# Projection operands by feature block: 256 tokens' high and low parts, then 320 tokens' high and low parts

## The chip, the cores and the metric

One core of a Trainium2 chip. The metric is device time in microseconds (us) of one execution, the median over several; "span" is the time from the first to the last instruction in the profiler's records of one execution. Engines: TensorE (PE; PEld is its loading of weights), VectorE (DVE), ScalarE (ACT), GpSimd (POOL) and SyncE (SP), which issues the transfers.

## The reference

One layer of a streaming encoder, in float32, on 512 prompt tokens and 64 sample tokens, with model width 1024:

```python
h = x + W_out [ GDN_group(n) ; DiffAttn_group(n) ]    # n = rmsnorm(x), one combined input projection of n
h = h + MemCrossAttn(rmsnorm(h), per-layer memory K/V)
h = h + W2 relu(W1 rmsnorm(h))^2
y = rmsnorm_final(h)
```

GDN is a gated delta rule over chunks of 64 tokens (four heads of 128 by 128 state) with a short convolution ahead; DiffAttn is causal attention by chunks with two softmax maps a head, of which the second is subtracted; MemCrossAttn attends to 256 memory rows with four heads of 256; the feed-forward layer has 4096 hidden features. Outputs are y and the new keys, values, states and memory projections.

## The kernel before

All 576 tokens (T; 512 of the prompt and 64 of the sample) are processed together, with features on the 128 partitions and tokens along the free dimension. Matmuls run in a reduced float32 form, so each weight and each input is kept as a high and a low part, and a product is made of three: high by high, high by low, low by high.

The inputs of a projection lie in tiles from `pair` (L79): 128 partitions by 2 parts by 4 feature blocks by 576 tokens, so that the low part of a feature block lies 4 x 576 columns behind its high part. Two such tiles hold the 1024 features of an input: xs for the normalised x, oa and ob for the outputs of the scan and of the diff attention, hx for the normalised h ahead of memory attention, mo for its output, fx for the input of the feed-forward layer, and one tile sx for each group of 512 hidden features.

`project` (L165) makes 128 output features of all tokens, in two halves of the tokens, `HALVES` = (0, 256) and (256, 320), each in one PSUM bank. For the first half, `high_parts` (L181) reads high and low of 256 tokens with one matmul of 512 columns, and a second matmul of 256 columns multiplies the low weights. For the second half three matmuls of 320 columns do it. This repeats for each of 8 feature blocks (4 in the second feed-forward matrix). After a half, the given `evac` adds the two halves of the bank and what else it has to do; `split_to` (L193) writes high and low parts of a result for a later projection: ScalarE casts the high part (L197), VectorE subtracts it from the source (L198), or with a gain the lines L200 and L201.

The stages, in time: projections of n (with `first_half`, L302, for the first ones), five groups of chunks of the scan, between which projections are laid, the last of them the sample's chunk ("the last scan chunk" below); then four diff-attention heads, during which the rest of the projections and then those of the memory keys and values (`wh` blocks by 512 weight columns, input as the stationary operand) fill TensorE; then the output projection w_out with the residual in hT, memory attention head by head (L1026 normalises a score row, L1044 and L1045 split its output, one PSUM bank g0 for the prompt tokens and one, g1, for the sample), the projection w_mem_o, and the feed-forward layer in 8 groups. Weights are loaded by SyncE into three `raw` buffers and split by ScalarE (L157) and VectorE (L158).

A scheduler of the framework orders the instructions of each engine from the program, by its own priorities and costs and by buffers coming free; `issue_after` and `keep_in_program_order` fix a few. So an instruction that is split in two also moves others. In the last scan chunk the lines are: L692 subtracts what the state predicts from the values (in the tile on), L697 forms the new values vn, L713 updates the state S, L718 to L724 normalise the chunk's output (again in a tile on), and the splits of oa follow it.

Of the kernel before, what the change touches and what calls it, by code (L numbers as in the profile page):

```python
# [15 lines left out]
P = 128  # L16
# [18 lines left out]
def hybrid_layer_kernel(  # L35
# [129 lines left out]
    def project(w, x, evac, kt=KT, halves=HALVES, between=None):  # L165


        for a0, n in halves:
            b = bank("pr")
            for k in range(kt):  # L170
                low_part = lambda: mm(b[:, :n], w[1][:, k, :], x[k // 4][:, 0, k % 4, a0 : a0 + n], start=False, stop=False)
# [20 lines left out]

    def split_to(x, src, k, a0, g=None):  # L193

        h, lo = (x[k // 4][:, j, k % 4, a0 : a0 + src.shape[-1]] for j in range(2))
        if g is None:
            A.copy(h, src)  # L197
            V.tensor_tensor(lo, src, h.bitcast(F32), ALU.subtract)  # L198
# [42 lines left out]
    xs = [pair(i, F32R) for i in (0, 1)]  # L241
    w2 = w_in[0]
    grow = small("B1", [1, 4 * P])
    grow2 = small("B1", [1, 4 * P])
# [35 lines left out]
    def hi(t, qs=(0, 1)):  # L280
        t0, n = TT[t]
        for q in qs:
            A.copy(xs[q][:, 0, :, t0 : t0 + n], turned[t][q])

    def lo(t, qs=(0, 1)):
        t0, n = TT[t]
        for q in qs:
            V.tensor_tensor(  # L288
                xs[q][:, 1, :, t0 : t0 + n], turned[t][q], xs[q][:, 0, :, t0 : t0 + n].bitcast(F32), ALU.subtract
            )  # L290

    class Parts(list):
# [9 lines left out]
    def first_half(m):  # L302

        b = bank("pr")
        for k in range(KT - 1):
            high_parts(b, wts[m][0], xs, k, 0, 256)
        for k in range(KT):
            mm(b[:, :256], wts[m][1][:, k, :], xs[k // 4][:, 0, k % 4, :256], start=False, stop=False)
        high_parts(b, wts[m][0], xs, KT - 1, 0, 256)
        return b  # L310

# [429 lines left out]
            project_z()  # L741
        S = gdn_scan(c, c0, t0, n, prepared[c], S)
    nc.sync.dma_start(o_gdn_s[0, 0].rearrange("h k v -> k h v"), S)
    oa = pair(2, F32R)
    for h in range(H):
        split_to((oa,), cq[:, h, :], h, 0)


    with tc.issue_after(opened[mybir.EngineType.DVE]):
# [143 lines left out]
        finish = diff_head(h, finish)  # L893
    finish()

    ob = pair(5, F32R)
    for h in range(H):
        split_to((ob,), od[:, h, :], h, 0)


    mkv = pair(1)
# [73 lines left out]
        return r2  # L975


    hx = [pair(i, F32R) for i in (4, 3)]
# [20 lines left out]
    for h in range(H):  # L999
        qh = [small("kd" if h % 2 else "aT", [P, T]) for i in range(2)]  # L1000
        for i in range(2):
            def scaled(b, a0, n, more):
                q = qh[i][:, a0 : a0 + n]
                if more is not None:
                    add_to(q, b, more)
                    b = q
                V.tensor_tensor(q, b, rB[:, a0 : a0 + n], ALU.mult)

            project(
                weights(w_mem_q[0], (2 * h + i) * P), hx, scaled,  # L1010
                between=broadcast if h == i == 0 else None,
            )
        pT = [small("p1" if h % 2 else "vb", [P, T]) for _ in range(2)]
        for t, (q0, _) in enumerate(QT):
            t0, n = TT[t]
            kk = mkT if t < 4 else cmT
            b = bank()
            for i in range(2):
                mm(b[:, :NMEM], qh[i][:, q0 : q0 + P], kk[:, 2 * h + i, :], start=i == 0, stop=i == 1)
            mx, l = tiny([P, 1]), tiny([P, 1])  # L1020
            V.tensor_reduce(mx, b[:, :NMEM], AX.X, ALU.max)
            V.tensor_scalar(mx, mx, -1.0 / 16, None, ALU.mult)
            p = small("p0", [P, 512])
            A.activation(p[:, :NMEM], b[:, :NMEM], AF.Exp, bias=mx, scale=1.0 / 16, accum_out=l)
            V.reciprocal(l, l)
            V.tensor_scalar(p[:, :NMEM], p[:, :NMEM], l, None, ALU.mult)  # L1026
            bt = bank()
            for bi in range(2):
                tr(bt[:, bi * P : (bi + 1) * P], p[:, bi * P : (bi + 1) * P])
            A.copy(pT[0][:, t0 : t0 + n], bt[:, P - n : P])  # L1030
            V.tensor_copy(pT[1][:, t0 : t0 + n], bt[:, 2 * P - n : 2 * P])
        if h % 2 == 0:
            mo.append(pair(4 if h else 5, F32R))
        for i in range(2):
            b, b2 = bank("g0"), bank("g1")
            fs = slice((2 * h + i) * P, (2 * h + i + 1) * P)
            for bi in range(2):
                mm(b, mv[:, bi, fs], pT[bi][:, :SEQ], start=bi == 0, stop=bi == 1)
            for bi in range(2):
                mm(b2[:, :DEC], cmv[:, bi, fs], pT[bi][:, SEQ:], start=bi == 0, stop=bi == 1)  # L1040
            j = 2 * (h % 2) + i
            for src, ts_ in ((b, slice(0, SEQ)), (b2[:, :DEC], slice(SEQ, T))):
                dh, dl = (mo[h // 2][:, p, j, ts_] for p in range(2))
                A.copy(dh, src)  # L1044
                V.tensor_tensor(dl, src, dh.bitcast(F32), ALU.subtract)  # L1045

    fx = [pair(i, F32R) for i in (3, 2)]
# [5 lines left out]

    NG = 8
    def ff1(g):
        sx = (pair((4, 1, 5)[g % 3], F32R),)
        for i in range(4):
            def evac(b, a0, n, more):
                f = small("fs", [P, 320])[:, :n]
                if more is not None:  # L1060
                    add_to(f, b, more)
                    b = f
                V.tensor_tensor(f, b, rB[:, a0 : a0 + n], ALU.mult)  # L1063
                V.scalar_tensor_tensor(f, f, 0.0, f, ALU.max, ALU.mult)  # L1064
# [132 lines left out]
```

## Time and profile before

| | before |
|---|---|
| median of 3 runs (us) | 1063.34 |
| lowest to highest (us) | 1062.84 to 1063.38 |
| profiled execution (us) | 1061.57 |
| its span (us) | 1059.5 |
| granted clock, mean | 0.996 |
| matmuls | 6574 |
| HBM traffic | 79.14 MB read, 9.74 MB written |

A line of a group gives source line, engine, operation, output and inputs by the program's names, shapes, the count after the x, then the busy time in us and the mean ns of one, and at the end the idle time of the engine just before such instructions with what ended it. A line of a timeline gives the start in us, the time from the first start to the last end of a run of equal instructions, and the same names; in brackets stands the idle time before it, and what ended it. Tiles of a pool are named without their numbers, and one slot's name, u, stands for most of the tiles from `pair`.

### The profile page before, as it was taken

To read this page: it belongs to the slowest core of one execution; us is meant where nothing else is said; L and a number is where in the kernel's file an instruction comes from. 1 tells how busy PE (TensorE), PEld (TensorE's weight loads), DVE (VectorE), ACT (ScalarE), POOL (GpSimd) and SP (SyncE) were. 2 spreads that over 40 slices of the span, in tenths; PEclk is the share of its full clock that TensorE was granted. 3 is DMA by queue.
4 is the path that set the end of the run, shared out by engine and by line. 5 is a ranking of instruction groups with operands and counts; after the bars stand their busy time and mean duration, and the time that the engine had idled before them with its cause. 6 is when DMAs were issued, how large, how long until landed. Compare 5 with 4: busy or idle time off the path is not lost.

```text
span 1059.5 us, 16941 instructions
## 1 busy us (share of the span) xinstructions
PE 1034.8 (98%) x6574; PEld 929.9 (88%) x6574; DVE 671.5 (63%) x1471; ACT 432.6 (41%) x897; POOL 73.8 (7%) x126
## 2 busy tenths in 40 slices
PE   8999899999999999999999999999999999999997
PEld 6999898898788877999887799999999999999996
DVE  6767684756467575564555666666666666666674
ACT  6644754333265665343333443323232323222344
POOL 4411120311000000000000000000000000000000
PEclk9999999999999999999999999999999999999998
DMA  7332310100132255524211122132414141323312
GB/s 212 116 120 78 114 41 21 42 1 22 54 88 63 89 179 198 166 80 140 60 41 40 57 83 63 58 100 60 116 47 124 44 119 50 110 59 109 91 51 90
DMA packets 139442, 89.96 MB, mean 85 GB/s; under 512 B 5522, under 2 KB 130576, under 8 KB 138852
## 3 DMA queue, kind: packets, MB, share of 16 engines
q1 hardware_dynamic: 138996, 88.24, 28.0%
q8 instruction: 52, 0.85, 0.3%
q10 hardware_dynamic: 368, 0.66, 0.2%
q14 instruction: 26, 0.21, 0.1%
HBM read 79.14 MB, written 9.74 MB: 84 GB/s over the span
## 4 chain that ended last, share of the span: by engine, by line
PE 90%; issue 4%; DVE 2%; ACT 2%; POOL 1%; DMA 0%; POOLq 0%; ACTq 0%; DVEq 0%
PE pr L103 70%; PE g L103 10%; PE gs L103 3%; PE ba L109 3%; PE ba L103 2%; PE g L109 2%; POOL tg L204 1%; POOL tiny L204 0%; PE pr L109 0%; PE gs L109 0%; ACT wh L157 0%; ACT u L1109 0%; ACT Y L656 0%; POOL u L630 0%; DVE on L724 0%
## 5 line engine op out<-in xcount | busy, mean ns | idle before, releaser
L103 PE MATMUL pr<-u,wh 128*128 128x512 f32 (+1 forms) x2664 | 699.5, 343 | 1.2 <-DVE u L288 0.9
L103 PEld LDWEIGHTS pr<-u,wh 128*128 128x128 f32 x2664 | 456.5, 188 | 37.8 <-issue 1.7
L103 PE MATMUL pr<-u,wl 128*128 128x256 f32 (+1 forms) x1776 | 484.7, 299 | 0.0
L103 PEld LDWEIGHTS pr<-u,wl 128*128 128x128 f32 x1776 | 328.4, 189 | 8.0 <-DVE wl L355 0.3
L157 ACT CAST wh<-raw 128x1024 fp32r<-128x1024 f32 (+1 forms) x153 | 136.5, 892 | 231.2 <-PE pr L103 212.4
L158 DVE TENSOR_TENSOR wl<-raw,wh 128x1024 fp32r<-128x1024 f32 (+1 forms) x153 | 157.4, 1029 | 61.3 <-ACT wh L157 59.5
L943 DVE TENSOR_TENSOR u<-u,pr 128x256 f32<-128x256 f32 (+1 forms) x160 | 72.3, 452 | 62.8 <-PE pr L103 60.2
L204 POOL TENSOR_TENSOR tiny<-tiny,nhalf 128x1 f32<-128x1 f32 (+4 forms) x11 | 10.1, 918 | 664.1 <-DVE tiny L1127 409.3
L197 ACT CAST u<-p 128x256 fp32r<-128x256 f32 x64 | 27.8, 435 | 51.8 <-DVE p L1064 51.8
L103 PE MATMUL pr<-wh,u 128*128 128x512 f32 x128 | 42.6, 405 | 0.0
L198 DVE TENSOR_TENSOR u<-p,u 128x256 fp32r<-128x256 f32 x64 | 29.2, 457 | 15.2 <-ACT u L197 15.2
L190 ACT COPY p<-pr 128x256 f32<-128x256 f32 (+1 forms) x44 | 16.4, 373 | 51.3 <-PE pr L103 51.3
L191 DVE TENSOR_TENSOR p<-pr,p 128x256 f32<-128x256 f32 (+1 forms) x44 | 18.6, 422 | 26.9 <-ACT p L190 26.9
L945 DVE TENSOR_TENSOR u<-u,pr 128x256 f32<-128x256 f32 x80 | 33.6, 420 | 2.4
L1063 DVE TENSOR_TENSOR p<-pr,rB 128x320 f32<-128x320 f32 x32 | 15.7, 492 | 25.7 <-PE pr L103 25.7
L415 DVE SCALAR_TENSOR_TENSOR p<-p,gcol,p 128x579 f32<-128x579 f32 x33 | 27.1, 821 | 6.4 <-ACT p L413 5.9
L1064 DVE SCALAR_TENSOR_TENSOR p<-p 128x256 f32<-128x256 f32 x64 | 29.3, 458 | 2.2
L665 ACT COPY X<-g 128x512 f32<-128x512 f32 (+1 forms) x24 | 13.2, 550 | 42.6 <-PE g L109 42.5
L200 ACT ACTIVATE u<-u,gcol 128x256 fp32r<-128x256 f32 (+1 forms) x32 | 17.0, 534 | 31.1 <-DVE u L945 31.1
L103 PE MATMUL g<-u,qz 128*128 128x256 f32 (+4 forms) x96 | 29.5, 411 | 0.0
L103 PEld LDWEIGHTS pr<-wh,u 128*128 128x128 f32 x128 | 23.6, 188 | 4.5 <-issue 0.2
L634 DVE SCALAR_TENSOR_TENSOR B<-lev,At 128x512 f32<-128x512 f32 (+1 forms) x30 | 20.7, 696 | 10.6 <-PE g L103 8.8
(317 smaller groups left out, 1211.8 us busy)
## 6 DMA issues: line engine op xcount, KB each, us to landing
raw<-in_w_ff_dram SPq DMA_DIRECT2D x32, 512.0 KB
raw<-in_w_ff_dram SPq DMA_DIRECT2D x64, 256.0 KB
raw<-in_w_in_dram SPq DMA_DIRECT2D x28, 512.0 KB
raw<-in_w_mem_k_dram SPq DMA_DIRECT2D x8, 512.0 KB
raw<-in_w_mem_v_dram SPq DMA_DIRECT2D x8, 512.0 KB
raw<-in_w_out_dram SPq DMA_DIRECT2D x8, 512.0 KB
raw<-in_w_mem_q_dram SPq DMA_DIRECT2D x8, 512.0 KB
raw<-in_w_mem_o_dram SPq DMA_DIRECT2D x8, 512.0 KB
```

Of the source, the lines that this page charges most:

```text
L103: i = nc.tensor.matmul(out, lhsT, rhs, start=start, stop=stop)
L109: i = nc.tensor.transpose(out, in_, ident[:n, :n])
L157: A.copy(wh, raw)
L158: V.tensor_tensor(wl, raw, wh.bitcast(F32), ALU.subtract)
L197: A.copy(h, src)
L198: V.tensor_tensor(lo, src, h.bitcast(F32), ALU.subtract)
L204: G.tensor_tensor(out, in_, bc(nhalf[: in_.shape[0], 0:1], list(in_.shape)), ALU.pow)
L415: V.scalar_tensor_tensor(yv[:, :n], cb[:, i : i + n], cwt[:, m, i : i + 1], yv[:, :n], ALU.mult, ALU.add)
L634: V.scalar_tensor_tensor(B[:n, :, :n], lev[:n, :n].unsqueeze(1).to_broadcast([n, 4, n]), float(lv), At[:n, :, :n], ALU.is_equal, ALU.mult,)
L943: V.tensor_tensor(hm, hm, b, ALU.add)
L945: V.tensor_tensor(hm, hm, more, ALU.add)
L1064: V.scalar_tensor_tensor(f, f, 0.0, f, ALU.max, ALU.mult)
```

## The change

A tile of a projection's inputs is now [128 partitions, 4 feature blocks, 1152 columns]. Within a feature block lie 256 tokens' high parts, the same tokens' low parts, 320 tokens' high parts and their low parts. The 512 columns that the first half's matmul reads are neighbours. `piece` finds a stretch of one part; a stretch may not cross from the first 256 tokens to the rest, so the splits of oa and ob, which took 576 tokens at once, are done by halves, and the split of a memory-attention output takes its 512 prompt tokens with one cast (which writes two separate pieces) and two subtracts.

```diff
+    def operand(slot):
+        return up.tile([P, 4, 2 * T], F32R, tag=f"u{slot}", name=nm("x"))
+
+    def piece(u, j, k, a0, n):
+        at = 256 * j + a0 if a0 < 256 else 512 + 320 * j + a0 - 256
+        return u[:, k, at : at + n]
...
     def high_parts(b, w, x, k, a0, n, kt=KT):
-        xk = x[k // 4][:, :, k % 4, a0 : a0 + n]
+        xk = x[k // 4]
         if a0 == 0:
-            mm(b.rearrange("p (j n) -> p j n", j=2), w[:, k, :], xk, start=k == 0, stop=k == kt - 1)
+            mm(b, w[:, k, :], xk[:, k % 4, :512], start=k == 0, stop=k == kt - 1)
         else:
-            mm(b[:, :n], w[:, k, :], xk[:, 0], start=k == 0, stop=False)
-            mm(b[:, :n], w[:, k, :], xk[:, 1], start=False, stop=k == kt - 1)
+            mm(b[:, :n], w[:, k, :], piece(xk, 0, k % 4, a0, n), start=k == 0, stop=False)
+            mm(b[:, :n], w[:, k, :], piece(xk, 1, k % 4, a0, n), start=False, stop=k == kt - 1)
...
     def split_to(x, src, k, a0, g=None):
-        h, lo = (x[k // 4][:, j, k % 4, a0 : a0 + src.shape[-1]] for j in range(2))
+        h, lo = (piece(x[k // 4], j, k % 4, a0, src.shape[-1]) for j in range(2))
...
-    oa = pair(2, F32R)
+    oa = operand(2)
     for h in range(H):
-        split_to((oa,), cq[:, h, :], h, 0)
+        for a0, n in HALVES:
+            split_to((oa,), cq[:, h, a0 : a0 + n], h, a0)
...
-    ob = pair(5, F32R)
+    ob = operand(5)
     for h in range(H):
-        split_to((ob,), od[:, h, :], h, 0)
+        for a0, n in HALVES:
+            split_to((ob,), od[:, h, a0 : a0 + n], h, a0)
...
-            for src, ts_ in ((b, slice(0, SEQ)), (b2[:, :DEC], slice(SEQ, T))):
-                dh, dl = (mo[h // 2][:, p, j, ts_] for p in range(2))
-                A.copy(dh, src)
-                V.tensor_tensor(dl, src, dh.bitcast(F32), ALU.subtract)
+            blk = mo[h // 2][:, j]
+            dh = blk[:, :1024].rearrange("p (c n) -> p c n", c=2)[:, :, :256]
+            A.copy(dh, b.rearrange("p (c n) -> p c n", c=2))
+            for a0 in (0, 256):
+                V.tensor_tensor(
+                    piece(mo[h // 2], 1, j, a0, 256), b[:, a0 : a0 + 256],
+                    piece(mo[h // 2], 0, j, a0, 256).bitcast(F32), ALU.subtract,
+                )
+            dh, dl = (piece(mo[h // 2], p, j, SEQ, DEC) for p in range(2))
+            A.copy(dh, b2[:, :DEC])
+            V.tensor_tensor(dl, b2[:, :DEC], dh.bitcast(F32), ALU.subtract)
...
```

The other tiles (xs, hx, fx, sx) change from `pair` to `operand`, and the lines that write or read them use `piece`. Lines behind the new functions have numbers higher by 7, later ones by up to 17.

Every projection keeps its matmuls and their number. The program order of the engines moves at three places. The first is VectorE in the last scan chunk. The rows of before, from L692 on (tg holds small factors, gs a bank of the scan, vb its values):

```order
L692 TENSOR_TENSOR on_2659<-vb_2487,gs_2654 64x512
L697 TENSOR_TENSOR vn_2666<-gs_2661,tg_2445 64x512
L719 TENSOR_REDUCE tg_2686<-on_2688 64x4
L720 TENSOR_TENSOR tg_2686<-tg_2686,tg_2478 64x4
L721 TENSOR_SCALAR tg_2686<-tg_2686 64x4
```

and of after (x_2703 is oa, u_78 holds the scan's output):

```order
L700 TENSOR_TENSOR on_2659<-vb_2487,gs_2654 64x512
L205 TENSOR_TENSOR x_2703<-u_78,x_2703 128x256 x4
L705 TENSOR_TENSOR vn_2666<-gs_2661,tg_2445 64x512
L727 TENSOR_REDUCE tg_2686<-on_2688 64x4
L728 TENSOR_TENSOR tg_2686<-tg_2686,tg_2478 64x4
```

Four subtracts of 256 tokens now stand between on and vn. On ScalarE the same stretch, before (u_2703 is oa; pr, zr and wh belong to projections between):

```order
L190 COPY u_78<-pr_3155 128x256
L718 ACTIVATE on_2688<-gs_2668 64x512
L157 CAST wh_3454<-raw_3452 128x1024
L190 COPY zr_3238<-pr_3221 128x256
L197 CAST u_2703<-u_78 128x576 x4
```

and after:

```order
L197 COPY u_78<-pr_3163 128x256
L204 CAST x_2703<-u_78 128x256 x4
L726 ACTIVATE on_2688<-gs_2668 64x512
L164 CAST wh_3462<-raw_3460 128x1024
L197 COPY zr_3246<-pr_3229 128x256
L204 CAST x_2703<-u_78 128x320 x4
```

The casts of the first 256 tokens stand ahead of the activation on the chunk's output, those of the rest where all stood.

The second place is TensorE from the end of the scan through the diff attention, where projection matmuls and attention matmuls are interleaved anew, with the same matmuls in all. The third is the last head of memory attention on TensorE, before (g_1088 and g_1090 are the bank g0 for the prompt tokens, p the probabilities, ba a transpose, pr_5902 the first bank of w_mem_o, u_5665 the first tile of mo):

```order
L103 MATMUL g_1088_5874<-p_1061_5792,u_4187 128x512
L103 MATMUL g_1088_5874<-p_1062_5793,u_4187 128x512
L109 MATMUL ba_5869<-ident,p_1086_5865 128x128 x2
L103 MATMUL g_1089_5875<-p_1061_5792,u_5025 128x64
L103 MATMUL g_1090_5884<-p_1061_5792,u_4187 128x512
L103 MATMUL g_1089_5875<-p_1062_5793,u_5025 128x64
L103 MATMUL g_1090_5884<-p_1062_5793,u_4187 128x512
L103 MATMUL g_1091_5885<-p_1061_5792,u_5025 128x64
L103 MATMUL g_1091_5885<-p_1062_5793,u_5025 128x64
L103 MATMUL pr_5902<-u_5665,wh_5898 128x512
```

and after (x_5685 is the first tile of mo):

```order
L110 MATMUL g_1088_5896<-p_1061_5814,u_4203 128x512
L110 MATMUL g_1088_5896<-p_1062_5815,u_4203 128x512
L116 MATMUL ba_5891<-ident,p_1086_5887 128x128 x2
L110 MATMUL g_1089_5897<-p_1061_5814,u_5041 128x64
L110 MATMUL pr_5926<-x_5685,wh_5922 128x512
L110 MATMUL g_1089_5897<-p_1062_5815,u_5041 128x64
L110 MATMUL pr_5926<-x_5685,wl_5923 128x256
L110 MATMUL pr_5984<-x_5685,wh_5980 128x512
L110 MATMUL g_1090_5907<-p_1061_5814,u_4203 128x512
L110 MATMUL g_1090_5907<-p_1062_5815,u_4203 128x512
L110 MATMUL g_1091_5908<-p_1061_5814,u_5041 128x64
L110 MATMUL g_1091_5908<-p_1062_5815,u_5041 128x64
```

Three matmuls of w_mem_o now stand ahead of the second use of bank g0.

More of the change, by code (lines that the diff above doesn't have):

```diff
@@ L170, in project @@
             for k in range(kt):
-                low_part = lambda: mm(b[:, :n], w[1][:, k, :], x[k // 4][:, 0, k % 4, a0 : a0 + n], start=False, stop=False)
+                low_part = lambda: mm(b[:, :n], w[1][:, k, :], piece(x[k // 4], 0, k % 4, a0, n), start=False, stop=False)
                 if k == kt - 1:
@@ L239, in turn @@
         return b.rearrange("p (i t) -> p i t", i=4)[:, :, :n]
-    xs = [pair(i, F32R) for i in (0, 1)]
+    xs = [operand(i) for i in (0, 1)]
     w2 = w_in[0]
@@ L282, in hi @@
         for q in qs:
-            A.copy(xs[q][:, 0, :, t0 : t0 + n], turned[t][q])
+            A.copy(piece(xs[q], 0, slice(0, 4), t0, n), turned[t][q])
     def lo(t, qs=(0, 1)):
@@ L288, in lo @@
             V.tensor_tensor(
-                xs[q][:, 1, :, t0 : t0 + n], turned[t][q], xs[q][:, 0, :, t0 : t0 + n].bitcast(F32), ALU.subtract
+                piece(xs[q], 1, slice(0, 4), t0, n), turned[t][q], piece(xs[q], 0, slice(0, 4), t0, n).bitcast(F32),
+                ALU.subtract,
             )
@@ L975, in norm_columns @@
         return r2
-    hx = [pair(i, F32R) for i in (4, 3)]
+    hx = [operand(i) for i in (4, 3)]
     for m in range(KT):
@@ L1032, in hybrid_layer_kernel @@
         if h % 2 == 0:
-            mo.append(pair(4 if h else 5, F32R))
+            mo.append(operand(4 if h else 5))
         for i in range(2):
@@ L1041, in hybrid_layer_kernel @@
             j = 2 * (h % 2) + i
-            for src, ts_ in ((b, slice(0, SEQ)), (b2[:, :DEC], slice(SEQ, T))):
-                dh, dl = (mo[h // 2][:, p, j, ts_] for p in range(2))
-                A.copy(dh, src)
-                V.tensor_tensor(dl, src, dh.bitcast(F32), ALU.subtract)
-    fx = [pair(i, F32R) for i in (3, 2)]
+            blk = mo[h // 2][:, j]
[9 more added lines that the diff above has]
+            V.tensor_tensor(dl, b2[:, :DEC], dh.bitcast(F32), ALU.subtract)
+    fx = [operand(i) for i in (3, 2)]
     for m in range(KT):
@@ L1055, in ff1 @@
     def ff1(g):
-        sx = (pair((4, 1, 5)[g % 3], F32R),)
+        sx = (operand((4, 1, 5)[g % 3]),)
         for i in range(4):
```

2 lines of the change are left out of this document (1 added, 1 removed).

## The prediction

> **What bounds the kernel now.** I read the page first: the busy shares, the chain that ended last and the granted clock.
>
> ```profile
> span 1059.5 us, 16941 instructions
> PE 1034.8 (98%) x6574; PEld 929.9 (88%) x6574; DVE 671.5 (63%) x1471; ACT 432.6 (41%) x897; POOL 73.8 (7%) x126
> PEclk9999999999999999999999999999999999999998
> PE 90%; issue 4%; DVE 2%; ACT 2%; POOL 1%; DMA 0%; POOLq 0%; ACTq 0%; DVEq 0%
> ```
>
> TensorE is busy for 98% of the span and makes 90% of the chain, at full clock in every slice. So the time changes only if a matmul of the same shape follows the one before it sooner, or if TensorE idles more or less. How much idle there is, and where, the windows say (window, length, then busy time of PE, PEld, DVE, ACT and POOL, the clock, the DMA share and GB/s):
>
> ```profile
> 285.00:431.00 146.00, 143.96 (x815) 118.71 (x814) 94.78 (x262) 85.36 (x240) 6.47 (x8) 1.00 0.40 126
> 515.00:594.00 79.00, 75.25 (x394) 58.87 (x394) 39.81 (x118) 26.64 (x74) 0.00 (x0) 1.00 0.12 34
> 636.00:1034.00 398.00, 397.37 (x2500) 373.18 (x2501) 261.69 (x517) 120.21 (x211) 1.17 (x1) 1.00 0.28 80
> ```
>
> TensorE idles 146.00 - 143.96 = 2.04 us from the last scan chunk's tail to the end of the memory projections, 79.00 - 75.25 = 3.75 us in memory attention, and 0.63 us in 398 us of feed-forward.
>
> **The 512-column read.** The groups by shape give the matmuls whose moving operand becomes contiguous (count after the x, then total us and mean ns; a mean includes pipeline latency and isn't the spacing). The last row is the matmul that alternates with them.
>
> ```profile
> L103 PE MATMUL pr<-u,wh 128*128 128x512 f32 x888 | 330.5, 402 | 0.9 <-DVE u L288 0.9
> L103 PE MATMUL pr<-u,u 128*128 128x512 f32 x32 | 10.8, 397 | 0.0
> L103 PE MATMUL pr<-u,wl 128*128 128x256 f32 x888 | 231.0, 287 | 0.0
> ```
>
> Sixteen more stand in the views of the tiles kd and wab, whose rows name the shapes at the end:
>
> ```profile
> L103 PE MATMUL pr<-u,kd x24: 309/309/503, 22.4 to 35.8; 128*128 128x320 f32 x16, 128*128 128x512 f32 x8
> ```
> ```profile
> L103 PE MATMUL pr<-u,wab x24: 305/309/398, 97.1 to 101.1; 128*128 128x320 f32 x16, 128*128 128x512 f32 x8
> ```
>
> That is 888 + 32 + 8 + 8 = 936 matmuls of 6574. None is added or removed. Each reads 256 high and then 256 low columns; before, the low ones lie 4 x 576 x 4 = 9,216 B behind, after, they follow at once. What a break in the middle costs shows where the trace has both kinds in a row. In the memory projections the moving operand is a weight block of 512 neighbouring columns; in the first projections the two-piece operand comes several times in a row (start, us from first start to last end, tiles, count):
>
> ```profile
> 412.01 0.62 PE L103 MATMUL pr<-wh,u 128*128 128x512 f32 x2
> ...
> 414.05 0.62 PE L103 MATMUL pr<-wh,u 128*128 128x512 f32 x2
> ```
> ```profile
> 18.68 1.08 PE L103 MATMUL pr<-u,wh 128*128 128x512 f32 x4
> 19.59 1.12 PE L103 MATMUL pr<-u,wl 128*128 128x256 f32 x8
> ```
>
> Contiguous: nine starts in 414.05 - 412.01 = 2.04 us, 226.7 ns each. In two pieces: these four matmuls end 1.08 us after the first began, and one alone takes 0.40, so (1.08 - 0.40) / 3 = 226.7 ns each. The same, so I price the break at 0. The 256-column ones are (1.12 - 0.28) / 7 = 120 ns apart, with 0.28 for one alone (a row at 109.83, below).
>
> In a projection the two shapes alternate, and there a pair should take 226.7 + 120 = 346.7 ns. The timeline of two projections, which read the same two-piece tiles:
>
> ```profile
> 103.64 0.40 PE L103 MATMUL pr<-u,wh 128*128 128x512 f32 x1
> ...
> 105.03 0.40 PE L103 MATMUL pr<-u,wh 128*128 128x512 f32 x1
> ```
> ```profile
> 109.59 0.40 PE L103 MATMUL pr<-u,wh 128*128 128x512 f32 x1
> 109.83 0.28 PE L103 MATMUL pr<-u,wl 128*128 128x256 f32 x1
> ...
> 111.36 0.40 PE L103 MATMUL pr<-u,wh 128*128 128x512 f32 x1
> ```
>
> The first runs four pairs in 1.39 us, 347.5 ns each; the second five in 1.77 us, 354.0 each. The second pace loses 354.0 - 346.7 = 7.3 ns a pair, and if that loss were the break, removing it would give at most 936 x 7.3 = 6.8 us. But the first keeps nearly the nominal pace with the same break. The loss comes from something else in a stream without bubbles, and I leave it where it is: term 0, other end -6.8.
>
> [...]
>
> **Splits by half, last scan chunk.** The splits of the scan's output (oa) become four casts and four subtracts of 256 tokens, then four of 320, and the program order places the first group inside the scan's last chunk: on VectorE between L692 (on) and L697 (vn), on ScalarE ahead of L718. What stands there now:
>
> ```profile
> 277.67 0.68 DVE L692 TENSOR_TENSOR on<-vb,gs 64x512 f32<-64x512 f32 x1 [0.19 <-PE gs L103]
> 279.76 0.68 DVE L697 TENSOR_TENSOR vn<-gs,tg 64x512 f32<-64x512 f32 x1 [1.41 <-PE gs L103]
> ```
> ```profile
> 280.20 0.45 PE L103 MATMUL pr<-u,wh 128*128 128x320 f32 x2
> 280.49 0.31 PE L103 MATMUL pr<-u,wl 128*128 128x320 f32 x1
> 280.73 0.43 PE L103 MATMUL gs<-S,u 128*64 128x128 f32 x2
> ```
> ```profile
> 283.72 0.59 ACT L718 ACTIVATE on<-gs 64x512 f32<-64x512 f32 x1 [6.70 <-PE gs L103]
> ```
> ```profile
> L197 ACT CAST u<-p 128x256 fp32r<-128x256 f32 x32 | 13.0, 407 | 44.7 <-DVE p L1064 44.7
> L198 DVE TENSOR_TENSOR u<-p,u 128x256 fp32r<-128x256 f32 x32 | 13.6, 426 | 15.2 <-ACT u L197 15.2
> ```
>
> VectorE idles 1.41 us before vn, and the four subtracts take 4 x 0.426 = 1.70 us. So vn starts 0.3 to 0.5 us late (the upper end with a gap between instructions), at about 280.2, and ends by 280.9. The matmul on S waits for vn and starts at 280.73 now; the new order puts two more 320-column matmuls ahead of it. Two start 280.49 - 280.20 = 0.29 us apart from what follows, so it wouldn't start before 280.73 + 0.29 = 281.02 anyway, and those two are work moved, not added. The cover is that 0.29 us; without it the stall would be 0.5. Term +0.1, ends 0 and +0.5. ScalarE's four casts (4 x 0.407 = 1.63 us) fall in the 6.70 us in which it waits before L718 now. The second group, of 320 tokens, stands where all four splits stood, and is first read with ob, below: 0.
>
> The split of ob, also by halves, ends near 405 us and is first read at 431.05; 25 us of memory projections hide it, so 0. If that cover were gone, four more subtracts would cost at most 4 x 0.426 = 1.7 us; the casts run beside them.
>
> ```profile
> 403.79 1.42 DVE L198 TENSOR_TENSOR u<-u,u 128x576 fp32r<-128x576 f32 x2
> ```
> ```profile
> 431.05 0.39 PE L103 MATMUL pr<-u,wh 128*128 128x512 f32 x1
> ```
>
> **The memory-attention output (mo).** One 512-column subtract becomes two of 256, eight times (group row; then who waited for that line, us and times):
>
> ```profile
> L1045 DVE TENSOR_TENSOR u<-g,u 128x512 fp32r<-128x512 f32 x8 | 5.5, 690 | 6.7 <-ACT u L1044 6.7
> ```
> ```profile
>   PEld g L103: 1.8, 5
> ```
>
> Each grows by 2 x 0.426 - 0.690 = 0.16 us. The bank g0 is one buffer, so the next 512-column matmul waits for it, as the 1.8 us in five waits show: at most 8 x 0.16 = 1.3 us. The new order of TensorE sets projection matmuls between the two bank turns, as in the last head, and the first half of the output projection needs only the earlier subtract, 0.26 us sooner (0.690 - 0.426): at least -0.3. I take +0.4, about half of the five waits growing.
>
> **The redrawn order.** From 288 to 403 us TensorE's rows are interleaved anew, because ScalarE and VectorE get other programs there. The work is the same, and only waits can change: a gain is bounded by the 2.04 us of idle time, a loss by the waits that could recur. Term 0. In the feed-forward stage the order of all engines is as before. On SyncE's queue a load of memory-key weights moves behind two output transfers, and the two reloads of hd move behind three outputs, and behind two outputs and a weight load:
>
> ```profile
> 322.09 0.43 SPq L153 DMA_DIRECT2D raw<-in_w_mem_k_dram  x1
> 323.39 0.38 SPq L807 DMA_DIRECT2D out_dram<-p  x1
> 323.87 0.48 SPq L810 DMA_DIRECT2D out_dram<-p  x1
> ...
> 372.67 0.58 SPq L934 DMA_DIRECT2D u<-hd  x1
> ```
> ```profile
> L157 ACT CAST wh<-raw x2: 1048/1054/1060, 331.3 to 348.0; 128x1024 fp32r<-128x1024 f32 x2
> ```
>
> The load is issued some 2 us later (323.87 + 0.48 - 322.09 = 2.26) and the next weight cast starts at 331.3, 7 us behind that; hd is the residual, needed after 431.05. Both 0; without the cover, the 2.26.
>
> **Sum.** 0 (pace) + 0.1 (chunk) + 0 (ob) + 0.4 (mo) + 0 (order) = +0.5 us. The profiled execution took 1061.57 us: its span of 1059.5 and 2.07 around it, 1.77 under the median of 1063.34. It would become 1062.1; carried to the median, **1063.8 us**. A measurement of this kernel can tell about 0.2%, 2.1 us, from no change.
>
> **Rivals.** *A, the break is the loss in the pairs:* the 512s start sooner everywhere, up to 6.8 us, so 1063.8 - 6.8 = 1057.0. For it: the loss is in nearly all projections. Against it: the run at 103 us and the equal 226.7 ns. Chance 0.15, a part of the gain included.
>
> *B, slower: the new order exposes a wait once in each of the four diff-attention heads.* The row to price it is the one such wait now (us, times, longest):
>
> ```profile
> PE ba L109 <- DVE an L878: 1.2, 1, 1.2
> ```
>
> TensorE runs its instructions in order. Where the filler of projection matmuls is spent earlier in a head, the transpose that waits for the normalised product (an) stands bare, as it does now only at the end. Three more heads give 3 x 1.24 = 3.7 us (its own row has 1.24 us), so 1067.5; it decides from two on, 2.5 us.
>
> ```profile
> 401.55 0.63 PE L109 MATMUL ba<-ident,an 128*128 128x128 f32 x4 [1.24 <-DVE an L878]
> ```
>
> For it: nothing in the change aims the new order at these waits. Against it: the filler is the same amount. Chance 0.26.
>
> *C, the new order fills idle time:* half of 2.04 + 3.75 us is 2.9, so 1060.9. For it: memory attention has the largest waits, and projection matmuls move into them. Against it: those waits come from softmax chains that the change doesn't shorten. Chance 0.11.
>
> That the change doesn't do its part needs no case: the columns do become neighbours, and my forecast is that TensorE takes no notice. Chance 0.48.
>
> **How the numbers follow.** Faster is A and C, 0.15 + 0.11 = 0.26; slower is B, 0.26; within 0.2% the forecast, 0.48. The range runs from A's end, 1057.0, to B's, 1067.5, which covers the bounds of the small terms (-0.3 to +1.8 about the median) and leaves out what lies beyond two or three exposed waits. The forecast's own range is 1062.0 to 1065.4.
>
> **What would show it.** Right: pairs in the feed-forward stage stay near the 354.0 ns of the second projection above, window 636:1034 lasts 398 us; vn starts 0.3 to 0.5 us after its old place relative to on; TensorE's idle time between the scan's tail and the memory projections stays within 2 us of 2.04. Wrong for A: pairs near 347 ns and a feed-forward window some microseconds shorter. Wrong for B: rows of waits on an, L878 or on weight casts counted four times instead of once. A span change over 2 us that lies in neither place would refute the list of terms itself.

## The result, and the profile after

The changed kernel takes 1062.59 us (median of 12 runs, 1060.55 to 1064.87) against 1062.93 (12 runs, 1061.31 to 1064.51): ratio 1.0001, 95% interval [0.9994, 1.0009] (the two medians alone give 0.9997). No change, as forecast. But it is no change in another way than the sum had it: as far as the profiles show, a gain that the sum carried at 0 and a loss that it had no term for cancel.

The page of after: span, busy shares, and the chain that ended last.

```profile
span 1061.8 us, 16966 instructions
PE 1037.3 (98%) x6574; PEld 933.5 (88%) x6574; DVE 673.3 (63%) x1487; ACT 433.7 (41%) x905; POOL 72.5 (7%) x126
PE 89%; issue 4%; DVE 3%; ACT 2%; POOL 1%; DMA 0%; POOLq 0%; ACTq 0%
```

The windows of after, where before had 143.96, 75.25 and 397.37 us of TensorE:

```profile
285.00:431.00 146.00, 144.04 (x821) 119.74 (x821) 94.25 (x265) 85.72 (x245) 6.06 (x8) 1.00 0.39 124
515.00:594.00 79.00, 75.55 (x387) 59.25 (x387) 39.04 (x123) 25.54 (x73) 0.00 (x0) 0.98 0.13 37
636.00:1034.00 398.00, 397.38 (x2503) 373.42 (x2502) 261.38 (x515) 119.67 (x210) 1.16 (x1) 1.00 0.28 81
```

One number is new: the granted clock of memory attention is 0.98.

Of the 2.3 us that the profiled execution of after is longer than that of before, 1.76 are there already at `on` in the last scan chunk (279.43 against 277.67, below). They aren't the change's: e10 below, in the same order, has `on` at 277.57, and e5, in the old order and layout, at 279.27. They come from the start: in the traces the first record of a clock of 1.00 stands at 18.37 us in after and at 12.61 in before, and the first 512s, at 15 to 17 us, are 427 ns apart in after and 227 in before. From `on` to w_out after then gains 0.90, and from w_out to the feed-forward stage it loses 1.66.

The projection that ran at 109.59 us before, now with neighbouring columns (timeline):

```profile
111.34 0.40 PE L110 MATMUL pr<-x,wh 128*128 128x512 f32 x1
111.58 0.28 PE L110 MATMUL pr<-x,wl 128*128 128x256 f32 x1
...
113.11 0.39 PE L110 MATMUL pr<-x,wh 128*128 128x512 f32 x1
```

Five pairs in 1.77 us, 354 ns each: as before, to the nanosecond that the rows show. VectorE in the last scan chunk:

```profile
279.43 0.68 DVE L700 TENSOR_TENSOR on<-vb,gs 64x512 f32<-64x512 f32 x1 [0.19 <-PE gs L110]
280.04 1.41 DVE L205 TENSOR_TENSOR x<-u,x 128x256 fp32r<-128x256 f32 x4
281.52 0.68 DVE L705 TENSOR_TENSOR vn<-gs,tg 64x512 f32<-64x512 f32 x1
```

From on to vn it is 2.09 us in both profiles (277.67 to 279.76 before): the four subtracts, 1.41 us from the first start to the last end, fit into the 1.41 us that were idle.

### The profile page after: what moved, and what is told of

Read it like the earlier page. It is cut to its first block, busy times and chain, and to the rows that moved or that the text cites. A ratio compares the mean times of both kernels' runs of the same rounds, so it can differ in the third digit from the quotient of the medians.

```text
span 1061.8 us, 16966 instructions
## 1 busy us (share of the span) xinstructions
PE 1037.3 (98%) x6574; PEld 933.5 (88%) x6574; DVE 673.3 (63%) x1487; ACT 433.7 (41%) x905; POOL 72.5 (7%) x126
## 4 chain that ended last, share of the span: by engine, by line
PE 89%; issue 4%; DVE 3%; ACT 2%; POOL 1%; DMA 0%; POOLq 0%; ACTq 0%
PE pr L110 69%; PE g L110 9%; PE gs L110 3%; PE ba L116 3%; PE ba L110 2%; PE g L116 2%; POOL tg L211 1%; DVE B L642 0%; DMA out_dram<-p 0%; POOL tiny L211 0%; PE pr L116 0%; DVE wl L165 0%; DVE Dt L669 0%; PE gs L116 0%; ACT wh L164 0%
## 5 line engine op out<-in xcount | busy, mean ns | idle before, releaser
L110 PE MATMUL pr<-x,wh 128*128 128x512 f32 (+1 forms) x2664 | 700.2, 344 | 1.1 <-DVE u L953 0.6
L110 PEld LDWEIGHTS pr<-x,wh 128*128 128x128 f32 x2664 | 457.5, 189 | 36.9 <-issue 1.1
L110 PE MATMUL pr<-x,wl 128*128 128x256 f32 (+1 forms) x1776 | 486.3, 300 | 0.0
L110 PEld LDWEIGHTS pr<-x,wl 128*128 128x128 f32 x1776 | 329.4, 189 | 8.4 <-issue 0.4
L204 ACT CAST x<-p 128x256 fp32r<-128x256 f32 x64 | 27.8, 434 | 51.8 <-DVE p L1081 51.8
L205 DVE TENSOR_TENSOR x<-p,x 128x256 fp32r<-128x256 f32 x64 | 29.2, 457 | 15.1 <-ACT x L204 15.1
L207 ACT ACTIVATE x<-u,gcol 128x256 fp32r<-128x256 f32 (+1 forms) x32 | 17.0, 534 | 30.7 <-DVE u L955 30.7
```

The costliest lines, as they stand in the source:

```text
L110: i = nc.tensor.matmul(out, lhsT, rhs, start=start, stop=stop)
```

## Experiments: is it two effects that cancel?

The theory on record (N): TensorE takes no notice of the break, and the order costs nothing. Its rival (C): the layout gains and the order loses as much. The first two kernels take the change apart.

**e1, the splits alone.** The old layout, with the new splits:

```diff
-        split_to((oa,), cq[:, h, :], h, 0)
+        for a0, n in HALVES:
+            split_to((oa,), cq[:, h, a0 : a0 + n], h, a0)
...
-                V.tensor_tensor(dl, src, dh.bitcast(F32), ALU.subtract)
+                for c in (0, 256) if src is b else (0,):
+                    e = slice(c, min(c + 256, src.shape[-1]))
+                    V.tensor_tensor(dl[:, e], src[:, e], dh[:, e].bitcast(F32), ALU.subtract)
```

> The old layout (low parts 9,216 B behind the high ones) with the changed kernel's splits: oa and ob by halves, two subtracts of 256 for a memory-attention output. PE, DVE, POOL and SP then stand in exactly the changed kernel's order. Theory N (TensorE takes no notice of the break, and the new order costs nothing): 1062.9 us, ratio 1.000 within 0.001. Rival C (the layout gains and the new order loses as much, so that they cancel in the changed kernel): slower, by at least 2 us, at most the 6.8 us of the pairs: 1065 to 1070.

Measured: 1062.43 us, ratio 0.9994 [0.9985, 1.0003].

**e2, the layout alone.** `operand` for xs, hx, fx and sx; oa, ob and mo stay `pair` and are split whole:

```diff
+        if len(u.shape) == 4:
+            return u[:, j, k, a0 : a0 + n]
         at = 256 * j + a0 if a0 < 256 else 512 + 320 * j + a0 - 256
...
-    oa = operand(2)
+    oa = pair(2, F32R)
```

> The new layout for xs, hx, fx and sx, the old one for oa, ob and mo, whose splits stay whole: 808 of the 936 matmuls of 512 columns read neighbouring columns, and every engine's order is that of before. Theory N: 1062.9 us, ratio 1.000 within 0.001, pairs at 353 to 354.5 ns as before. Rival C: faster by at least 2 us and up to 808 x 7.3 ns = 5.9 us: 1057 to 1061.

Measured: 1062.43 us, ratio 0.9998 [0.9989, 1.0007]. Rival C wanted e1 slower by 2 us and e2 faster by 2; both are out. The layout is worth nothing that this can resolve. The order isn't quite nothing, though. VectorE's `on` in the last chunk and the first matmul of w_out, in e1 and then in e2:

```profile
277.68 0.68 DVE L692 TENSOR_TENSOR on<-vb,gs 64x512 f32<-64x512 f32 x1 [0.19 <-PE gs L103]
...
430.11 0.39 PE L103 MATMUL pr<-u,wh 128*128 128x512 f32 x1
```
```profile
277.79 0.68 DVE L709 TENSOR_TENSOR on<-vb,gs 64x512 f32<-64x512 f32 x1 [0.19 <-PE gs L112]
...
431.23 0.39 PE L112 MATMUL pr<-u,wh 128*128 128x512 f32 x1
```

With the new order this stretch takes 430.11 - 277.68 = 152.43 us, with the old one 153.44 (and 431.05 - 277.67 = 153.38 in before). The new order gains 0.95 us here. It isn't one execution's luck: in the five full-rate profiles with the new splits (after, e1, e8, e10, e12) the stretch takes 152.38 to 152.72 us, in five that keep the old order there (before, e2, e5, e9, e11) 153.33 to 153.44.

## Experiments: what does a break cost?

**e3, single elements.** High and low parts of a token side by side, so that every matmul of a projection reads every second element:

```diff
-        at = 256 * j + a0 if a0 < 256 else 512 + 320 * j + a0 - 256
-        return u[:, k, at : at + n]
+        v = u[:, k, 2 * a0 : 2 * (a0 + n)]
+        return v.rearrange("p (n j) -> p j n", j=2)[:, j]
```

> High and low parts interleaved token by token: the 512-column matmul reads the same 4 KB-wide stretch in two passes with every second element, so 256 short pieces a pass instead of one break; the 256- and 320-column ones read every second element too, and ScalarE and VectorE write so. Order of the engines as in the changed kernel. Theory N taken to its end (the moving read's pieces cost nothing): 1063 us, pairs near 353 ns. Theory P (each piece costs, and one break was just too little to see): 512-column matmuls grow; if a read of every second element halves the rate, 512 columns take 213 ns longer, 936 x 0.213 = 199 us for these alone, and over 400 us with the 320- and 256-column ones. Anything between dates the price of a piece.

Measured: 1731.0 us, ratio 1.6285 [1.6262, 1.6307]. The timeline of its feed-forward stage:

```profile
1201.15 0.64 PE L110 MATMUL pr<-x,wh 128*128 128x512 f32 x1
1201.61 0.41 PE L110 MATMUL pr<-x,wl 128*128 128x256 f32 x1
1201.84 0.64 PE L110 MATMUL pr<-x,wh 128*128 128x512 f32 x1
```

512 columns take 0.46 us (1201.61 - 1201.15) and 256 take 0.23, where before has 0.227 and 0.120: half the rate. That is 0.23 us more for a 512; the 213 ns of the expectation is twice the 226.7 - 120 = 106.7 ns that 256 columns more take in before. So TensorE does take notice of pieces; theory N holds for one break in 512 columns, not for any layout. Two more kernels ask for the length from which it is free. They differ from e3 in the piece, `"p (c j e) -> p j c e"` with e = 2 in e7, e = 4 in e8, and in that the prompt tokens of a memory-attention output are subtracted at once.

> High and low parts interleaved two tokens by two: the matmuls read pieces of 2 elements (8 B) with 8 B left out between them. If each piece costs, whatever its length, the loss is half of that with single elements: 1063 + 334 = about 1397 us. If the read goes by lines of 16 B and each line costs the same whether used whole or half: as with single elements, 1731 us. If it goes by 8 B: 1063 us.

> The same, four tokens by four: pieces of 4 elements, 16 B. If each piece costs: a quarter of the loss with single elements, 1063 + 167 = 1230 us. If the read goes by lines of 16 B or of 8 B: 1063 us. If by more than 16 B: 1731 us or near it.

Measured, one run each: 1731.94 us with pieces of 8 B, 1060.6 us with pieces of 16 B. Whole groups of e7, then of e8:

```profile
L115 PE MATMUL pr<-x,wh 128*128 128x512 f32 x888 | 565.5, 640 | 1.2 <-DVE x L301 1.2
```
```profile
L115 PE MATMUL pr<-x,wh 128*128 128x512 f32 x888 | 328.1, 399 | 1.0 <-DVE x L301 1.0
```

The count of pieces doesn't set the time (that would have given 1397 and 1230): e7 has half as many as e3 and takes as long, 1731.94 us against 1731.0, and e8 has a quarter of them and takes no longer than before. Of the readings on record only the one by 16 B gives both times. The two times agree with it; how the read is done, they don't show. All pieces of e8 start at a multiple of 16 B within their tile; other starts weren't tried. The pieces of the old layout were 1,024 B, 64 times those of e8, and e2, which does without the break in 808 of the 936 matmuls, has 0.9998: there was nothing to gain.

## Experiments: where do the 7 ns of a pair come from?

**e4, grouped.** In the first half of each projection, all 512s but the last, then all 256s, then the last 512 (old layout):

```diff
+            for k in range(kt - 1 if a0 == 0 else 0):
+                high_parts(b, w[0], x, k, a0, n, kt)
             for k in range(kt):
...
-                high_parts(b, w[0], x, k, a0, n, kt)
+                if a0 or k == kt - 1:
+                    high_parts(b, w[0], x, k, a0, n, kt)
```

> The kernel before, with the first half of each projection in another order of its matmuls: the 512-column ones of all feature blocks but the last, then all the 256-column ones, then the last 512, so that the shapes change 3 times in a projection of 8 blocks instead of 15. It asks where the 7.3 ns of a pair come from. Theory S (they are paid where the shape changes): up to 936 x 7.3 = 6.8 us faster, and about half of that, 1059.5, if a run of 512s first has to settle, as the 230, 236, 229, 232, 231, 227 ns of a run at 97 us suggest. Theory B (they belong to each 512 in a stream without bubbles, whatever stands beside it): 1062.9, pairs' sum unchanged.

Measured: 1064.06 us, ratio 1.0013 [1.0004, 1.0021]: slower, where theory S wanted up to 6.8 us less. Yet its dense projections are shorter, as S has it: 6.32 us from one to the next,

```profile
599.76 2.07 PE L103 MATMUL pr<-u,wh 128*128 128x320 f32 x9
...
606.08 2.07 PE L103 MATMUL pr<-u,wh 128*128 128x320 f32 x9
```

where the kernel before takes (616.66 - 597.62) / 3 = 6.347 for a projection of 8 blocks, and (708.99 - 702.64) / 2 = 3.175 for one of 4:

```profile
597.62 0.28 PE L103 MATMUL pr<-u,wl 128*128 128x256 f32 x1
...
616.66 0.28 PE L103 MATMUL pr<-u,wl 128*128 128x256 f32 x1
...
702.64 0.28 PE L103 MATMUL pr<-u,wl 128*128 128x256 f32 x1
...
708.99 0.28 PE L103 MATMUL pr<-u,wl 128*128 128x256 f32 x1
```

So grouping the shapes takes away about half of the pairs' loss, and something else takes the gain away. **e5** groups only w_out, w_mem_o from its second block on, and the feed-forward matrices, so that the scan and the diff attention keep their order. (The last head of memory attention doesn't quite: the wait ahead of the one of 1.98 us is 1.28 us there, 0.57 in before.)

> The kernel before with the 512s grouped only where TensorE runs nothing but projections: the 8 of w_out, 7 of w_mem_o, the 32 of the first feed-forward matrix (8 blocks each) and 56 of the second (4 blocks each). Theory S, as the last run's timeline sizes it (6.32 us a projection of 8 blocks where it took 6.347, 3.160 one of 4 where it took 3.175): 47 x 0.027 + 56 x 0.015 = 2.1 us faster, 1060.9, ratio 0.998, with no loss, since the stages that lost by it (scan and memory attention) keep their order. Rival: grouping costs waits here too, and nothing is gained: 1063.

Measured: 1063.43 us, ratio 1.0005 [0.9996, 1.0015]. Nothing again, though its projections of 4 blocks take 704.37 - 701.21 = 3.16 us instead of 3.175:

```profile
701.21 0.69 PE L103 MATMUL pr<-u,wh 128*128 128x512 f32 x3
...
704.37 0.69 PE L103 MATMUL pr<-u,wh 128*128 128x512 f32 x3
```

**e6, two 256s** in place of a 512 for all inner blocks:

```diff
+            if 0 < k < kt - 1:
+                mm(b[:, :256], w[:, k, :], xk[:, 0], start=False, stop=False)
+                mm(b[:, 256:], w[:, k, :], xk[:, 1], start=False, stop=False)
```

> The kernel before, with two matmuls of 256 columns (high, then low) in place of one of 512, for all feature blocks but the first and last of a projection: the break inside the instruction is gone, and there is no change of shape between them, at the price of one more instruction each. Theory S: three 256s take 3 x 120 = 360 ns where a pair took 353 to 354.5, so some 6 ns a block more, about 640 blocks, +4 us. If the loss of a pair were in the break: the same three would still take 360, so the total can't tell these two; but if the loss goes with any stream without bubbles, three take 366 ns or more.

Measured, one run: 1071.35 us, +8.8 where +4 was expected. The timeline bears the 360 ns out (two blocks from 701.26 to 701.98); most of the rest lies ahead of the last scan chunk, whose `on` starts at 288.12 us instead of 277.67, and I didn't follow it further.

```profile
701.26 0.28 PE L103 MATMUL pr<-u,wl 128*128 128x256 f32 x1
701.38 0.40 PE L103 MATMUL pr<-u,wh 128*128 128x256 f32 x2
701.62 0.29 PE L103 MATMUL pr<-u,wl 128*128 128x256 f32 x1
...
701.98 0.40 PE L103 MATMUL pr<-u,wl 128*128 128x256 f32 x2
```

## Experiments: the clock behind a wait

The windows around the last memory-attention head show what ate the gains (length, TensorE's busy time, granted clock), of before, after, and e5 in this order:

```profile
580.00:592.00 12.00, 8.92 (x39) 1.00 0.01 1
```
```profile
580.00:592.00 12.00, 8.88 (x33) 0.86 0.00 1
```
```profile
580.00:592.00 12.00, 8.42 (x23) 0.72 0.01 1
```

In single microseconds of after, the clock is 1.00 while TensorE stands still, and 0.50 from 584.98 on, where TensorE happens to start again:

```profile
583.00:584.00 1.00, 0.00 (x1) 1.00 0.00 0
584.00:585.00 1.00, 0.02 (x1) 0.99 0.00 0
585.00:586.00 1.00, 1.00 (x4) 0.50 0.06 16
586.00:587.00 1.00, 1.00 (x4) 0.50 0.00 0
587.00:588.00 1.00, 1.00 (x3) 0.50 0.00 0
588.00:589.00 1.00, 1.00 (x3) 0.80 0.00 0
```

Three whole microseconds at 0.50, 0.4 more in the one at 0.80 and 0.02 at 0.99 make 3.42 us at half clock. In e5, 12 us at a mean of 0.72 are 6.7 us of it, twice as long. Ahead of the fall stands this in the timeline of after: some 1.0 us of scores, and then a wait of 1.98 us for a normalised score row.

```profile
581.97 1.03 PE L110 MATMUL ba<-u,kd 128*128 128x256 f32 x4
584.98 0.66 PE L116 MATMUL ba<-ident,p 128*128 128x128 f32 x2 [1.98 <-DVE p L1036]
585.43 1.92 PE L110 MATMUL ba<-u,kd 128*128 128x256 f32 x4
```

The wait of before is just as long and its profile has no fall there. It has one earlier, though: from 130 to 140 us the clock is 0.83 in before, after, e1, e2, e5 and e8, and from 128 to 140 us it is 0.86 in e11 and e12; in e4, e9 and e10 it is 1.00 there. So the mean clock of a run counts the falls and doesn't place them; one fall of 3.41 us takes 0.0016 off it. Before has 0.995 to 0.997 in 78 of its 82 runs beside e1 to e12; after has 0.994 in nine of 12, and e1, in the same order, in six of 11. That is about one fall more in most executions of the new order. That it is the one in memory attention, the profile of after shows for one execution; for the runs without a profile it isn't shown.

Where the falls of before and after stand can be read from the clock in their traces. All its changes in one of these executions lie whole multiples of 3.413 us apart: in after the falls begin at 134.42, 584.98 and 1056.02, 132 and 138 steps apart, in before at 132.07 and 1053.67, 270 steps. Here is TensorE's busy time in the step ahead of the fall in after, and in the two steps around the same wait in before:

```profile
581.57:584.98 3.41, 1.28 (x6) 1.00 0.00 0
```
```profile
579.22:582.63 3.41, 2.38 (x13) 1.00 0.00 0
582.63:586.05 3.42, 1.90 (x8) 1.00 0.02 5
```

In before the edge of a step cuts the wait in two, and neither step is as empty. In these two executions each of the five falls from full clock follows a step with 1.28 to 1.40 us of matmuls (1.37, 1.28 and 1.39 in after, 1.35 and 1.40 in before), and the emptiest step at full clock that none follows is the one with 1.90 us above. Two executions don't make that a threshold. Where the edges lie differs between them (the first record of 1.00 stands at 12.61 us in before, 18.37 in after), and the wait of 1.98 us brought a fall in the profile of after and none in those of before and of e1, which has the order of after (1.00 from 580 to 592 us). The edges would explain that; it isn't shown. Why the new order should meet more falls stays open.

The next kernels fill the wait: matmuls that repeat the last scores into an unused bank, held behind them in the order.

```diff
+            for _ in range(6 if (h, t) == (H - 1, 3) else 0):
+                ...
+                mm(spare[:, :NMEM], qh[0][:, q0 : q0 + P], kk[:, 2 * h, :])
```

> The kernel before, with six more score matmuls of 256 columns (0.257 us each, into a spare bank, never read) in the wait of 1.98 us in the last memory-attention head. Theory G (where TensorE stands still there, the granted clock falls to 0.50 for some microseconds in some executions, which is 2 us of time, and the orders differ in how often): the mean clock of each run at 0.996 or above, median 1062.4, since before falls seldom; no fall in the profile between 575 and 600 us. Rival: the fillers only lengthen the chain, 1062.9 or up to 1064.5.

Measured: 1062.94 us, ratio 1.0001 [0.9993, 1.0010]; the expected 0.4 us didn't come. Its profile has a clock of 1.00 from 580 to 592 us, no fall, as expected, but six of the 11 runs have a mean clock of 0.995 where every one was to have 0.996 or above; that would fit a fall at 130 us in these, which the fillers can't reach. And the fillers were too long: each is two passes of 0.215 us, 2.6 us for six, and the transposes start 3.45 us behind the scores ahead (581.05 to 584.50) where before takes 3.00 (581.15 to 584.15).

> The changed kernel with the same six matmuls in the same wait. Its runs had a mean clock of 0.994 in 9 of 12 (1061.9 to 1064.9 us) and 0.996 in two (1060.55, 1062.08). Theory G: clock 0.996, median 1061.3, ratio 0.9985. Rival (the falls follow from something else, and the fillers change nothing): clock 0.994, 1062.6.

Measured: 1060.9 us, ratio 0.9984 [0.9975, 0.9993], all 11 runs at a clock of 0.996 to 0.998: as theory G had it. (Its profile has no fall at 130 us either, ahead of any filler; that one is worth some 0.5 us: from the matmul at 110.89 in before it is 166.78 us to `on`, from the same one in e10, at 111.33, 166.24.) The same stretch of its profile, with the fillers in the bank gs:

```profile
580.00:592.00 12.00, 11.52 (x55) 1.00 0.01 1
```
```profile
580.87 2.75 PE L110 MATMUL gs<-u,kd 128*128 128x256 f32 x12
583.46 0.38 PE L116 MATMUL ba<-ident,p 128*128 128x128 f32 x2
```

> The kernel with grouped 512s in the dense stages, with nine fillers, three in the wait ahead (1.28 us) and six in the one of 1.98 us. Its runs were at a clock of 0.992 or 0.993 in 10 of 12 (1062.6 to 1065.4) and 0.996 in two (1059.72, 1061.95). Theory G with theory S: the 2.1 us of grouping come out, 1060.5, ratio 0.998 or lower. Rival: the gain of grouping was lost in waits, not in the clock: 1063.

Measured: 1061.58 us, ratio 0.9986 [0.9977, 0.9995]: with the clock held in memory attention (1.00 from 580 to 592 us in its profile) the grouped kernel gains 1.2 us by the medians, of the 2.1 that were expected; its fillers are too long as well.

**e12** puts together what was measured apart: the changed kernel, the grouping in the dense stages, four fillers.

> The changed kernel, with the 512s grouped in w_out, w_mem_o from its third block of outputs on, and the feed-forward matrices, and with four filler matmuls in the wait of 1.98 us (each is two passes of 0.215 us in the trace, so six of them were 0.4 us too long for the wait, and four fit). If the three sizes add up as measured apart (new order -0.95 us up to w_out, grouping -1.9, no fall of the clock in memory attention, nothing for the fillers), 1062.8 becomes 1059.9, ratio 0.9973. Rival: they overlap or the clock falls all the same: 0.9984 as with the fillers alone.

Measured: 1058.25 us (7 runs), ratio 0.9965 [0.9954, 0.9976]. It is faster than before, and its interval lies below that of after; the sum's 0.9973 lies inside it. That the sum comes out isn't shown part by part. In its profile the order gives 1.0 us (152.38 against 153.38 to w_out) and the feed-forward stage 3.1 (from its first matmul with low weights to the last of 256 columns 378.54 against 381.66), while the stretch from w_out to the feed-forward stage loses 1.0 (206.10 against 205.10). Its fillers end inside the wait, of which 0.26 us is left:

```profile
580.87 1.89 PE L110 MATMUL gs<-u,kd 128*128 128x256 f32 x8
583.01 0.41 PE L116 MATMUL ba<-ident,p 128*128 128x128 f32 x2 [0.26 <-DVE p L1048]
```

## Why the prediction was right, point by point

- **Pace, 0:** right, and for the reason given. Pairs are at 354 ns after as before, and e2 gives 0.9998. In the feed-forward stage the median projection takes 6.347 us with 8 blocks and 3.173 with 4 in before, after and e2 alike. The row that priced the two-piece read shows the last four of seven matmuls in a row; all seven, from the first start to the next shape, take 19.59 - 17.90 = 1.69 us in before and 19.66 - 17.96 = 1.70 with neighbouring columns in e2. The loss of a pair isn't the break. Grouping removes about half of it (e4, e5), and e6's three equal shapes take 360 ns a block without any; but e8 removes nearly as much with the shapes alternating (6.327 and 3.160 us), so what causes it stays open. Rival A is out.
- **Last scan chunk, +0.1:** measured 0. The step that priced the subtracts at 4 x 0.426 = 1.70 us took the duration of lone ones; in a row the four took 1.41 us together, which is the idle time that was there. The two projection matmuls ahead moved the matmul on S as forecast: it starts 3.34 us behind `on` instead of 3.06, in work that was moved.
- **ob, 0:** nothing of it shows; counted from `on`, w_out starts no later in any full-rate kernel with the new splits (152.38 to 152.72 us behind it, against 153.38 in before).
- **mo, +0.4:** measured 0. From the transposes behind the long wait to the second projection of w_mem_o, past both uses of bank g0, before takes 597.62 - 584.15 = 13.47 us and e1, with the two subtracts and the clock held, 596.66 - 583.17 = 13.49. Of the five waits that I let grow, 1.8 us in before, none is left: in after and in e1 nothing is shown to wait for the subtract of an output. The projection matmuls that the order put between the two uses of the bank would explain that; no kernel takes them away.

```profile
584.15 0.41 PE L109 MATMUL ba<-ident,p 128*128 128x128 f32 x2 [1.98 <-DVE p L1026]
```
```profile
583.17 0.41 PE L109 MATMUL ba<-ident,p 128*128 128x128 f32 x2 [1.98 <-DVE p L1028]
...
596.66 0.28 PE L103 MATMUL pr<-u,wl 128*128 128x256 f32 x1
```

- **Order, 0:** mis-sized. It gains 0.95 us up to w_out, and TensorE's idle time there is the same (2.04 us before, 1.96 after), so the gain lies in how matmuls of the two kinds follow one another, not in waits that the profile names. Which switches it is stays open. Rival B's waits didn't appear: the wait on an is counted once in after, as before. That TensorE took its instructions in order there, before's trace shows at the row that priced B: it stands still for 1.24 us to 401.55, and a matmul at 402.36, whose low weights VectorE had split by 396.72 + 1.23 = 397.95 us, comes behind the transposes. The prediction's rival C, idle time filled by the order, is out too: besides those 1.96 us, memory attention idles 79.00 - 75.55 = 3.45 us in after and 3.75 before.
- **What the sum had no term for:** the clock. The prediction read full clock in every slice off the row PEclk. But a 9 there stands for 90% or more, and the last digit is an 8: before's own clock is 0.83 from 130 to 140 us. So what a redrawn order does to the clock was put at nothing without a reason. In the profile of after it falls in memory attention, and the mean clocks speak for one more fall in most executions. From the transposes to the first sample matmuls after takes 5.46 us (584.98 to 590.44) and e10, in the same order at full clock, 3.88 (583.46 to 587.34): 1.6 us. Against the 0.95 of the order that leaves a result within the interval of 1. The forecast of no change stands on a right price for its main term and on two misses that cancel, and that they cancel is luck.

```profile
590.44 0.43 PE L110 MATMUL g<-p,u 128*128 128x64 f32 x2 [0.57 <-ACT p L1040]
```
```profile
587.34 0.44 PE L110 MATMUL g<-p,u 128*128 128x64 f32 x2 [0.30 <-ACT p L1049]
```

That the fall is what keeps after from being faster than before is borne out by e10, which adds nothing but the fillers and comes out at 0.9984, while the same fillers change nothing in before (e9, 1.0001). Its interval, 0.7 to 2.7 us, holds the 0.95 of the order; the fillers' excess of 0.4 us should have taken part of that. The missing fall at 130 us in its profile, 0.5 us, could make it up; whether the runs without a profile lack it too isn't shown.

## What to carry to other kernels

Before a layout is changed for contiguity, look in the trace for the same shape read both ways in a row: here both had 226.7 ns, and the layout alone (e2) then bore it out. In the layouts tried here pieces of 1,024 B (before, 226.7 ns for 512 columns) and of 16 B with 16 B between them (e8, 1060.6 us) cost nothing that shows, and pieces of 4 and of 8 B, with as much between them, halved the rate (e3 and e7, 1731.0 and 1731.94 us). And a gain of two microseconds stayed away where the clock fell: of the 2.1 us expected of e5 none came (1.0005, 6.7 us at half clock in its profile), and 1.2 came with the wait filled (e11, 0.9986). So read the granted clock next to the longest wait, in windows of a microsecond and not in slices of the span, and try to fill that wait with matmuls if it falls behind it.

## What the runs showed of the hardware that I had not expected

- TensorE stood still for 1.98 us, shortly after a wait of 0.57, and came back at half clock for 3.4 us in the profile of after, where 1.28 us of a 3.413 us step of the clock were busy. In that of before, with the same waits, it didn't: there the step's edge cut the wait (2.38 and 1.90 us busy). With the wait filled it is gone in the profile (0.86 in after, 1.00 in e10, from 580 to 592 us).
- Reading 4 B of every 8 (e3), or 8 B of every 16 (e7), halved the rate at which the matmuls took their moving operand (512 columns in 0.46 us instead of 0.23; 1731.0 and 1731.94 us in all); reading 16 B of every 32 (e8) left it at 0.23 and cost nothing that one run shows (1060.6 us). VectorE, which writes the same pieces, didn't slow: its shortest subtract of 256 columns in the feed-forward stage takes 425 ns in e3 and 424 in before.
- With pieces of 16 B (e8) a projection of 4 blocks takes 703.38 - 700.22 = 3.16 us in the one profile, as short as with the grouped order, though its shapes alternate. Why a finer address pattern should shorten the alternation stays open.

```profile
700.22 0.40 PE L115 MATMUL pr<-x,wl 128*128 128x256 f32 x2
...
703.38 0.40 PE L115 MATMUL pr<-x,wl 128*128 128x256 f32 x2
```
